# A two-layer decoder trunk on one core: the first stage arranged anew between the two modulation halves, one reading engine for each PSUM bank, and the norm's gain folded into the output weights

## The chip, the core and the metric

The kernel runs on one core of one Trainium2 chip. The metric is the device time of one execution in microseconds (us), as a median over runs; lower is better. The core's engines in the profile are PE (TensorE: matrix products and transposes, with PEld loading its weights), DVE (VectorE), ACT (ScalarE), POOL (GpSimd) and SP (SyncE, which here only issues DMAs). Each engine works through its own row of instructions in order.

## The reference, cut to what matters

```python
for l in range(2):                                   # x: 1024 tokens x 1024
    shift, scale, gate = split(silu(c) @ w_mod[l] + b_mod[l])
    h = rms_norm(x, pre_gain[l]) * (1 + scale) + shift
    proj = h @ w_in[l]                               # 3088 columns
    aq, ak, av, ag, rq, rk, rv, rg, gq, gk, gv, gg, ga = split(proj)
    a_out = sliding_window_attention(rot(aq), rot(ak), av, sinks[l]) * silu(ag)
    r_out = rms_norm(retention(rot(rq), rot(rk), rv)) * silu(rg)
    g     = gated_linear_attention(gq, gk, gv, log_sigmoid(ga @ gw + gb) / 16)
    g_out = rms_norm(g, gla_norm_gain[l]) * silu(gg)  # gain: 64 values, the same for 4 heads
    y = concat(a_out, r_out, g_out) @ w_out[l]        # the last 256 rows of w_out meet g_out
    x = x + gate * rms_norm(y, post_gain[l])
```

`rot` turns pairs by the angle position x frequency; its sine and cosine come from tables that the kernel makes itself.

## The kernel before

**Tiles and products.** Tokens are worked in eight tiles of 128. The columns of W_in are cut into units of 256 (`gg` with the 16 columns of `ga` beside it is 272 wide; then `rg`, `rq`, `rk` and so on; W_out is `o0` to `o3`). Each fp32 operand is held as a high and a low part, and a product of one tile with one unit is three passes (high x high, low x high, high x low) over 8 slices of 128 rows: 24 matmuls at L161 into one PSUM bank. High parts are made by a copy (L473, L475, L577), low parts by subtracting the high part from the original (L478, L561, L581).

**PSUM.** Of the eight banks three are for products (`mm`) and five for transposes and the rest (`aux`); a fourth product has to wait until the readers of the first are done.

**The first stage** (`mod_first`). The modulation of layer 0 needs shift and scale, 1024 values each, from 8 MB of `w_mod`. They come in two halves `hh` of 512 columns. In each half eight row slices `wm` arrive by DMA; PE makes the shift row (`mm<-wm,c_act`), DVE adds up the scale (`acc`; L322 for the first slice, L324 for the others). `finish(hh)` turns both into columns with eight small matmuls against ones, and L304 to L306 on DVE complete them. Only then can the normalised, transposed tiles 0 and 1 be modulated (L571 on ACT, L573 on DVE), split and multiplied. `between(hh, k)` is called after slice k and puts other work there: loading `gg`'s weights ahead of half 1's slices, normalising tiles 0 and 1 (`pre`), loading tiles 2 and 3.

**What follows.** `gg` and `rg` of tiles 0 and 1, then of the pairs 2/3, 4/5, 6/7. `gla_logits` turns a `gg` product into its gate: `silu2` is tanh on ACT (L880) and one DVE operation (L882); a further DVE multiply (L889) puts the norm's gain on it, a DMA stores it, and ACT copies the 16 `ga` columns (L892). The sine and cosine tables are a job (`table_job`, `tables`) of nineteen steps, nearly all on DVE (L411 to L439; two sines on ACT, L435 and L436), that is let in between the gates' steps.

**What sets the order.** PE's order is written by a planner in the code: a clock `clk` adds up matmul costs, jobs are generators that yield a delay from the table `L` or the name of a flag, and `pump()` lets the due ones issue. The other engines take their instructions in the order in which a scheduler puts them, and the two queues that issue DMAs (SP and ACT) are in order too. A DMA also waits for the landing of the one eight before it. `B2` is the number of 2 KB buffers (`t2`), 13; `BST` the number of staging buffers for weights, 5.

## Time and profile before

| | before |
|---|---|
| median of 3 runs | 1011.76 us (1010.34 to 1012.52) |
| the profiled execution | 1013.59 us |
| its span, first to last instruction | 1011.7 us |
| mean granted clock of TensorE | 0.971 |
| busy: PE / DVE / ACT / POOL | 972.2 / 653.4 / 377.4 / 279.7 us |
| matmul and transpose instructions on PE in the profile | 7185 |

The profile shows one execution. Its own time is 1.89 us above its span and 1.83 us above the median of the runs. A row of the timeline gives start, length, engine, source line, operation, output<-inputs and count, and in brackets how long the engine had been idle before and what released it. The granted clock is the share of full speed at which TensorE's array runs.

### The profile page before, as it was taken

What the parts mean: (1) busy time and instruction counts of PE and PEld (TensorE: products, weight loads), DVE (VectorE), ACT (ScalarE), POOL (GpSimd) and SP (SyncE); (2) the same over time, 40 slices, a digit from 0 to 9 for tenths busy, and PEclk for the clock granted to TensorE, in tenths of its full rate; (3) what the DMA queues carried; (4) which work ended last, traced back from release to release, by engine and by line L of the source; (5) the groups of instructions that cost most, each with busy time, mean ns of one, the idle gap of its engine ahead of it and who ended that gap; (6) DMA issues with size and microseconds to landing.
All of it is one profiled execution on the core that took longest, in us unless ns stands there. A gap on an engine that the chain in (4) does not pass through costs nothing.

```text
span 1011.7 us, 19347 instructions
## 1 busy us (share of the span) xinstructions
PE 972.2 (96%) x7185; PEld 845.3 (84%) x7185; DVE 653.4 (65%) x1565; ACT 377.4 (37%) x1050; POOL 279.7 (28%) x310
## 2 busy tenths in 40 slices
PE   5898999999999999999999999999999999999997
PEld 1588999988998877778889999998899887777886
DVE  3789956767757687654478495686575577753322
ACT  2465421232322466632254432132332256662111
POOL 2342201332432154521225120133233124541000
PEclk8899999999899999999999999999988999999999
DMA  9841522443325245678555160153132214455653
GB/s 320 292 123 33 177 69 76 123 130 97 115 86 175 53 138 157 201 246 275 181 166 185 48 183 16 58 168 105 53 95 85 92 46 151 131 164 189 222 189 143
DMA packets 124153, 140.44 MB, mean 139 GB/s; under 512 B 12462, under 2 KB 95384, under 8 KB 124060
## 3 DMA queue, kind: packets, MB, share of 16 engines
q1 hardware_dynamic: 116060, 127.50, 41.0%
q10 hardware_dynamic: 8000, 11.72, 3.3%
q8 instruction: 56, 0.92, 0.4%
q14 instruction: 37, 0.30, 0.1%
HBM read 102.48 MB, written 34.60 MB: 136 GB/s over the span
## 4 chain that ended last, share of the span: by engine, by line
PE 78%; DVE 10%; DMA 5%; ACT 3%; issue 3%; POOL 1%; SPq 0%; ACTq 0%; DVEq 0%; POOLq 0%
PE mm L161 61%; PE aux L161 12%; PE aux L176 4%; DMA st<-in_w_mod_dram 1%; DVE t L573 1%; DVE arena L478 1%; ACT smx L812 1%; POOL sm L514 1%; DMA mixS<-t 1%; DMA xk<-in_x_dram 1%; DMA t<-t 1%; DVE t L544 1%; DVE acc L361 0%; DMA c_freq<-cst_freq_dram 0%; DVE arena L147 0%
## 5 line engine op out<-in xcount | busy, mean ns | idle before, releaser
L161 PE MATMUL mm<-arena,arena 128*128 128x256 f32 (+2 forms) x1824 | 299.9, 320 | 7.1 <-DVE t L882 4.0
L161 PE MATMUL mm<-arena 128*128 128x256 f32 (+2 forms) x1824 | 299.1, 321 | 5.4 <-ACT arena L577 3.0
L161 PEld LDWEIGHTS mm<-arena,arena 128*128 128x128 f32 x1824 | 258.6, 193 | 31.0 <-DVE t L882 4.4
L161 PEld LDWEIGHTS mm<-arena 128*128 128x128 f32 x1824 | 260.7, 195 | 27.9 <-ACT arena L577 3.2
L161 PE MATMUL mm<-arena,mx 128*128 128x512 f32 (+1 forms) x816 | 179.9, 380 | 0.0
L161 PEld LDWEIGHTS mm<-arena,mx 128*128 128x128 f32 x816 | 146.1, 188 | 30.0 <-issue 0.8
L514 POOL TENSOR_TENSOR sm<-sm,mhalf 128x1 f32<-128x1 f32 (+1 forms) x64 | 55.0, 859 | 320.2 <-DVE sm L513 315.8
L478 POOL TENSOR_TENSOR arena<-st,arena 128x512 fp32r<-128x512 f32 x66 | 96.2, 1465 | 102.4 <-ACT arena L145 60.4
L145 ACT ACTIVATE t<-aux 128x512 f32<-128x512 f32 (+1 forms) x96 | 48.4, 519 | 91.2 <-PE aux L161 49.1
L816 POOL TENSOR_TENSOR smx<-smx,sm 128x512 f32<-128x512 f32 x32 | 35.6, 1113 | 112.9 <-DVE sm L815 97.0
L478 DVE TENSOR_TENSOR arena<-st,arena 128x512 fp32r<-128x512 f32 x62 | 61.1, 999 | 4.0 <-PE mm L161 1.7
L145 ACT ACTIVATE arena<-st 128x512 fp32r<-128x512 f32 x90 | 52.5, 624 | 27.3 <-PE mm L161 13.8
L361 DVE SCALAR_TENSOR_TENSOR acc<-st,c_act,acc 128x512 f32<-128x512 f32 x60 | 48.2, 803 | 14.4 <-DMA st<-in_w_mod_dram 13.4
L812 ACT ACTIVATE smx<-smx,sm 128x129 f32<-128x129 f32 x128 | 50.1, 393 | 18.2 <-DVE sm L809 18.0
L176 PE MATMUL aux<-c_ident,t 128*128 128x128 f32 x288 | 47.3, 291 | 7.5 <-DVE t L544 4.4
L1119 ACT ACTIVATE t<-mm 128x512 f32<-128x512 f32 x30 | 18.0, 599 | 93.7 <-PE mm L161 42.6
L1120 DVE TENSOR_TENSOR t<-mm,modg 128x512 f32<-128x512 f32 x30 | 20.7, 688 | 48.8 <-ACT t L1119 48.8
L1155 DVE SCALAR_TENSOR_TENSOR t<-t,sm,t 128x512 f32<-128x512 f32 x32 | 23.8, 777 | 37.1 <-DMA t<-xs 18.8
L176 PEld LDWEIGHTS aux<-c_ident,t 128*128 128x128 f32 x288 | 35.8, 148 | 12.4 <-DVE t L544 5.6
L145 ACT ACTIVATE t<-mm 128x256 f32<-128x256 f32 x40 | 14.9, 379 | 73.6 <-PE mm L161 30.6
L161 PEld LDWEIGHTS aux<-t,mx 32*128 32x128 f32 (+1 forms) x896 | 39.7, 188 | 2.1 <-issue 1.2
L161 PE MATMUL aux<-t,mx 32*128 32x32 f32 (+1 forms) x896 | 40.6, 272 | 0.0
(191 smaller groups left out, 1225.9 us busy)
## 6 DMA issues: line engine op xcount, KB each, us to landing
st<-in_w_in_dram SPq DMA_DIRECT2D x96, 256.0 KB, 3.1
st<-in_w_mod_dram SPq DMA_DIRECT2D x64, 256.0 KB, 3.3
mx<-mixS SPq DMA_DIRECT2D x32, 512.0 KB, 6.5
mixS<-t SPq DMA_DIRECT2D x64, 128.0 KB, 2.7
st<-in_w_out_dram SPq DMA_DIRECT2D x32, 256.0 KB, 2.9
mixS<-t SPq DMA_DIRECT2D x32, 256.0 KB, 2.9
wm<-in_w_mod_dram SPq DMA_DIRECT2D x12, 512.0 KB, 6.1
t<-in_x_dram SPq DMA_DIRECT2D x24, 256.0 KB, 4.6
```

Of the source, the lines that this page charges most:

```text
L145: A.activation(dst, src, AF.Copy)
L161: T.matmul(dst, lhsT, rhs, start=start, stop=stop)
L176: T.transpose(dst, src, idn)
L361: V.scalar_tensor_tensor(acc, wt, c_act[:, k:k + 1], acc, ALU.mult, ALU.add)
L478: (G if first == 0 else eng(f"wlo{kc}")).tensor_tensor(wt[:, 1, 2 * kc:2 * kc + 2, 0:256], st, f(hi), ALU.subtract)
L514: G.tensor_tensor(r, r, mhalf[:, :w], ALU.pow)
L544: V.tensor_scalar(xn[j], xt[j], r, None, ALU.mult)
L812: A.activation(sm[:, h, :], sm[:, h, :], AF.Exp, bias=mx[:, h:h + 1], accum_out=sums[:, h:h + 1])
L816: eng("pn").tensor_tensor(sm[:, :, 0:128], sm[:, :, 0:128], rs.unsqueeze(2).to_broadcast((P, 4, P)), ALU.mult)
L1119: A.activation(yg, pm, AF.Square, accum_out=ss[:, nh:nh + 1])
L1120: V.tensor_tensor(yg, pm, modg[l][:, 512 * nh:512 * nh + 512], ALU.mult)
L1155: V.scalar_tensor_tensor(xt[j], yg[j], r, xt[j], ALU.mult, ALU.add)
```

## The change

1. `load` takes the list of 256-row pieces. `gg`'s first two pieces and its 16 `ga` columns are loaded ahead of half 1's slices, the other two behind them; the low parts of the latter are made on DVE instead of POOL.
2. `between` steps the table generator (`tab`, by the counts in `TAB_N`): eleven steps in half 0, eight in half 1. `table_job` is left with the transposes of the tables.
3. At slice 5 of half 1 `begin` issues eight of the 24 products of `gg` for each of tiles 0 and 1 (high part of `h`, slices 0 to 3); `complete` issues the other sixteen of each after half 1.
4. `pre_early` replaces the early branch of `pre`. Transposes go into four banks: A0, A1 (first halves of tiles 0 and 1) and A2 are read by ACT alone, V2 by DVE alone. ACT modulates slices 4 and 5 and copies their high part, DVE slices 6 and 7 with a copy of its own. The low parts of the first halves (`rest`) are made after half 1's last addition.
5. `rg`'s weights are loaded ahead of x of tiles 2 and 3, and all four of their high parts are made on ACT.
6. In all other `pre`s ACT modulates the first half and DVE the second (`TURN`); before, one slice of the first half and two of the second were ACT's.
7. The multiply by the norm's gain (L889, 16 of them over both layers) goes. The gain is loaded as a column `gncol`, halved, and multiplied into the last two row slices of each unit of W_out while they are split: in the scale of ACT's copy, and in a DVE operation for the low part (eight of them; POOL made them before).
8. `gla_logits` copies `ga` ahead of the tanh. `B2` is 12 instead of 13, and about half of the delays in `L` have other values.

```diff
@@ mod_first
+        rest(0)
         finish(1, row, acc)
@@ load
-    def load(l, name, first=None):
+    def load(l, name, first=None, kcs=range(KT // 2)):
...
+            if name[0] == "o" and kc == 3:
+                gain = gncol[:, l:l + 1]
+                A.activation(hi, st, AF.Copy, scale=gain)
+                V.scalar_tensor_tensor(wt[:, 1, 6:8, 0:256], st, gain, f(hi), ALU.mult, ALU.subtract)
+                continue
             if first == 0:
                 A.activation(hi, st, AF.Copy)
+            elif first == 1 and kc in RG_V:
+                V.tensor_copy(hi, st)
             elif first == 1:
-                V.tensor_copy(hi, st)
+                A.activation(hi, st, AF.Copy)
...
-            (G if first == 0 else eng(f"wlo{kc}")).tensor_tensor(...)
+            (G if first == 0 and kc < 2 else V if first == 0 else eng(f"wlo{kc}")).tensor_tensor(...)
@@
+    def early_products(t, seq, start, stop):
+        w, h = unit(0, "gg"), hT[(0, 0)]
+        c = slice(t * P, t * P + P)
+        for i, (a, b, k) in enumerate(seq):
+            mult(begun[t][:, 0:272], h[:, a, k, c], w[:, b, k, 0:272], start and i == 0, stop and i == len(seq) - 1)
+
+    def begin(t):
+        begun[t] = mm()
+        early_products(t, [(0, b, k) for b in range(2) for k in range(4)], True, False)
+
+    def rest(t):
+        with tc.issue_after(mark[2].ins):
+            V.tensor_tensor(*half.pop(t), ALU.subtract)
+
+    def complete(t):
+        early_products(t, [(1, 0, k) for k in range(4)], False, False)
+        early_products(t, [(a, b, k) for a, b in ((0, 0), (0, 1), (1, 0)) for k in range(4, 8)], False, True)
@@ pre
-                if (j == 0 or k % 2 if early else k in TURN_ACT[j]):
+                if TURN[l][j] == "A":
@@
+    def pre_early(t, xn, h):
+        if t == 0:
+            turns.update({n: aux() for n in ("A0", "A1", "A2", "V2")})
+        for k in range(8):
+            bank = turns[f"A{t}" if k < 4 else "A2" if k % 4 < 2 else "V2"]
...
+        yield (0.0, ("modh", 0, 0))
+        hf = t2()
+        for k in range(4):
+            modulate(A, hf[:, k * P:(k + 1) * P], turns[f"A{t}"][:, k * P:(k + 1) * P], k)
...
+        yield (0.0, ("modh", 0, 1))
+        if t:
+            rest(1)
+        los = []
+        for e, n, k0 in ((A, "A2", 4), (V, "V2", 6)):
...
@@ between
+        for _ in range(TAB_N[8 * hh + k] if k >= 0 else 0):
+            next(tab, None)
+        if hh == 1 and k == BEGIN:
+            begin(0)
+            begin(1)
         if hh == 0 and k == -1:
-            load(0, "gg", 0)
+            load(0, "gg", 0, range(2))
...
         elif hh == 1 and k == -1:
-            for t in (2, 3):
-                load_x(t, xe[t], nc.sync)
+            load(0, "gg", 0, range(2, 4))
@@
+    with tc.issue_after(mark[0].ins), tc.issue_after(mark[1].ins):
+        load(0, "rg", 1)
+    for t in (2, 3):
+        load_x(t, xe[t], nc.sync)
...
-    with tc.issue_after(mark[0].ins), tc.issue_after(mark[1].ins):
-        load(0, "rg", 1)
@@
-    gn5 = cp.tile([P, 2, 64], F32, name="gn5")
...
+    for j in range(2):
+        nc.sync.dma_start(gncol[64 * j:64 * j + 64, :], gn_in.rearrange("a b -> b a"))
+    V.tensor_scalar(gncol, gncol, 0.5, None, ALU.mult)
@@ gla_logits
-        sg = silu2(pg)
-        so = t1()
-        eng("gso").tensor_tensor(h4(so), h4(sg), gn5[:, l].unsqueeze(1).to_broadcast((P, 4, 64)), ALU.mult)
-        dma("ssg", sgS[t], so)
         ga = small(16)
         A.activation(ga, pa, AF.Copy)
+        dma("ssg", sgS[t], silu2(pg))
@@ table_job
-        yield L["tb1"]
-        for _ in tables():
+        for _ in tab:
             yield L["tb2"]
         flag("tables", 2.0)
+        yield L["tb1"]
@@
-B2, B1, BS, BST, MMB, SMB = 13, 8, 11, 5, 3, 6
+B2, B1, BS, BST, MMB, SMB = 12, 8, 11, 5, 3, 6
-TURN_ACT = ((2,), (0, 3))
+TURN = ("AV", "AV")
-L = {"tt1": 6.37, ... "tb1": 24.85, "tb2": 0.52, ... "pf1": 11.01, ... "kv1": 3.07, "kv2": 0.96, ... "fin1": 7.77, ... "pre1@1": 7.74, ...}
+L = {"tt1": 6.51, ... "tb1": 26.69, "tb2": 0.05, ... "pf1": 9.58, ... "kv1": 8.31, "kv2": 2.31, ... "fin1": 11.68, ... "pre1@1": 9.85, ...}
+TAB_N = (0, 1, 1, 2, 1, 1, 1, 1, 2, 2, 1, 3, 0, 0, 0, 0)
+BEGIN = 5
+RG_V = ()
```

Four pieces of the order of instructions. Lines moved with the edits: L544, L571, L573, L577, L473, L478, L880, L882 and L892 of before are, for the early tiles or in general, L573, L613, L614, L621/L635, L479/L483, L486, L944, L946 and L952 of the change, and the table's lines moved by one.

PE around half 1, before (`mm_228` is half 1's shift row, `mm_247` and `mm_285` the columns of halves 0 and 1, `mm_410` and `mm_444` `gg` of tiles 0 and 1, `mm_478` and `mm_508` `rg` of them):

```order
L161 MATMUL mm_228<-wm_224,c_act 1x512 x2
L161 MATMUL mm_247<-c_ones,t_14_122 128x1 x4
L161 MATMUL mm_247<-c_ones,row_123 128x1 x4
L161 MATMUL mm_228<-wm_224,c_act 1x512 x6
L161 MATMUL mm_285<-c_ones,t_42_226 128x1 x4
L161 MATMUL mm_285<-c_ones,row_227 128x1 x4
L161 MATMUL mm_410<-arena_71 128x272 x24
L161 MATMUL mm_444<-arena_71 128x272 x24
L161 MATMUL mm_478<-arena_318,arena_71 128x256 x24
L161 MATMUL mm_508<-arena_318,arena_71 128x256 x7
```

The same stretch now (`mm_232` the shift row, `mm_258` and `mm_323` the columns, `mm_299` and `mm_308` `gg`, `mm_503` and `mm_533` `rg`):

```order
L161 MATMUL mm_232<-wm_228,c_act 1x512 x2
L161 MATMUL mm_258<-c_ones,t_14_123 128x1 x4
L161 MATMUL mm_258<-c_ones,row_124 128x1 x4
L161 MATMUL mm_232<-wm_228,c_act 1x512 x4
L161 MATMUL mm_299<-arena_71 128x272 x8
L161 MATMUL mm_308<-arena_71 128x272 x8
L161 MATMUL mm_232<-wm_228,c_act 1x512 x2
L161 MATMUL mm_323<-c_ones,t_43_230 128x1 x4
L161 MATMUL mm_323<-c_ones,row_231 128x1 x4
L161 MATMUL mm_299<-arena_71 128x272 x16
L161 MATMUL mm_308<-arena_71 128x272 x16
L161 MATMUL mm_503<-arena_361,arena_71 128x256 x24
```

Sixteen of the 48 products of `gg` now stand ahead of half 1's last two slices.

DVE from half 0's columns to half 1's columns, before (`t_42_226` is half 1's `acc`):

```order
L304 TENSOR_TENSOR sm_256<-mm_247,sm_169 128x4
L324 SCALAR_TENSOR_TENSOR t_42_226<-wm_225,c_act,t_42_226 128x512
L305 SCALAR_TENSOR_TENSOR mod_11_119<-sm_256,sm_169 128x4
L306 TENSOR_TENSOR mod_10_118<-mm_247,sm_165 128x4
L324 SCALAR_TENSOR_TENSOR t_42_226<-wm_225,c_act,t_42_226 128x512 x6
L561 TENSOR_TENSOR arena_71<-t_47_260,arena_71 128x4x128
L304 TENSOR_TENSOR sm_294<-mm_285,sm_169 128x4
```

And now, from behind half 0's columns to half 1's (`t_43_230` is half 1's `acc`, `t_48_254` and `sincos` the tables):

```order
L430 SCALAR_TENSOR_TENSOR t_48_254<-t_40_225,t_48_254 128x512 x2
L324 SCALAR_TENSOR_TENSOR t_43_230<-wm_229,c_act,t_43_230 128x512
L430 SCALAR_TENSOR_TENSOR t_48_254<-t_40_225,t_48_254 128x512
L324 SCALAR_TENSOR_TENSOR t_43_230<-wm_229,c_act,t_43_230 128x512
L432 TENSOR_SCALAR t_48_254<-t_48_254 128x512
L324 SCALAR_TENSOR_TENSOR t_43_230<-wm_229,c_act,t_43_230 128x512
L438 SCALAR_TENSOR_TENSOR sincos<-sincos 128x8x64
L324 SCALAR_TENSOR_TENSOR t_43_230<-wm_229,c_act,t_43_230 128x512
L440 TENSOR_SCALAR sincos<-sincos 128x8x64
L324 SCALAR_TENSOR_TENSOR t_43_230<-wm_229,c_act,t_43_230 128x512 x2
L549 TENSOR_TENSOR arena_71<-t_51_271,arena_71 128x4x128
L549 TENSOR_TENSOR arena_71<-t_52_277,arena_71 128x4x128
```

Six steps of the tables stand between the additions to `acc`; behind the last row come two low parts of `gg`'s weights (L486), and then half 1's columns.

DVE at the first gates, now (`sm_401` is the norm of tile 3, `t_87_477` the gate of `mm_299`, whose bank `mm_533` takes):

```order
L573 TENSOR_SCALAR t_70_394<-mx_115,sm_401 128x512
L573 TENSOR_SCALAR t_71_395<-mx_115,sm_401 128x512
L946 SCALAR_TENSOR_TENSOR t_87_477<-t_86_475,mm_299 128x256
L946 SCALAR_TENSOR_TENSOR t_90_500<-t_89_498,mm_308 128x256
L946 SCALAR_TENSOR_TENSOR t_93_530<-t_92_528,mm_503 128x256
```

The three gates stand behind the normalisation of both tiles; before, the first of them (L882) stood ahead of tile 3's.

DVE a little later, where tiles 2 and 3 are modulated, now (`t_98_558` and `t_102_582` are their second halves):

```order
L844 COPY smx_4440<-sink_441 128x4
L591 TENSOR_SCALAR t_98_558<-aux_553,mod_11_120,mod_10_119 128x128 x3
L745 TENSOR_SCALAR gncol<-gncol 128x2
L591 TENSOR_SCALAR t_98_558<-aux_553,mod_11_120,mod_10_119 128x128
L591 TENSOR_SCALAR t_102_582<-aux_577,mod_11_120,mod_10_119 128x128 x3
L596 TENSOR_TENSOR arena_71<-t_98_558,arena_71 128x4x128
L591 TENSOR_SCALAR t_102_582<-aux_577,mod_11_120,mod_10_119 128x128
L946 SCALAR_TENSOR_TENSOR t_104_608<-t_103_606,mm_533 128x256
```

The halving of `gncol`, which waits for the two small DMAs, stands among the modulations; `gn5`'s halving stood there before.

80 lines of the change are left out of this document (49 added, 31 removed).

## The prediction, as it stood before the changed kernel was run

> **What bounds the kernel now.** I read the page's head first, then busy time by stretch, PE's timeline with what released it, and last the other engines' rows at the places where PE waits.
>
> ```profile
> PE 972.2 (96%) x7185; PEld 845.3 (84%) x7185; DVE 653.4 (65%) x1565; ACT 377.4 (37%) x1050; POOL 279.7 (28%) x310
> 75.00:100.00 25.00, 22.14 (x168) 20.24 (x168) 22.76 (x50) 13.47 (x32) 4.79 (x4) 1.00 0.10 33
> 150.00:500.00 350.00, 343.69 (x2620) 295.78 (x2619) 235.98 (x562) 130.78 (x383) 107.92 (x126) 0.98 0.48 146
> 500.00:1012.00 512.00, 501.13 (x3694) 442.16 (x3692) 308.36 (x733) 181.12 (x511) 132.72 (x143) 0.98 0.40 125
> ```
>
> PE is the bound: 972.2 of 1011.7 us. Columns of the other rows: stretch, length, busy time of PE, PEld, DVE, ACT and POOL, PE's granted clock, DMA share, GB/s. The change issues as many products as before, so it can gain only where PE idles or runs at a low clock. From 150 us on PE idles 6.3 and 10.9 us, spread thin. Between 75 and 100 us DVE is fuller than PE (22.76 against 22.14): there DVE is the limit. PE's own rows show the places:
>
> ```profile
> 22.45 5.10 PE L161 MATMUL mm<-wm,c_act 128*1 128x512 f32 x8
> 41.64 7.73 PE L161 MATMUL mm<-arena 128*128 128x272 f32 x44 [2.97 <-ACT arena L577]
> 49.22 3.00 PE L161 MATMUL mm<-arena,arena 128*128 128x256 f32 x25
> 51.83 1.07 PE L161 MATMUL mm<-arena,arena 128*128 128x256 f32 x8
> 59.23 4.80 PE L161 MATMUL mm<-arena 128*128 128x272 f32 x24 [2.46 <-ACT sm L892]
> 63.90 3.27 PE L161 MATMUL mm<-arena 128*128 128x272 f32 x24
> 80.86 2.65 PE L161 MATMUL mm<-arena,arena 128*128 128x272 f32 x16 [0.80 <-POOL arena L581]
> 95.03 3.27 PE L161 MATMUL mm<-arena,arena 128*128 128x272 f32 x24 [1.89 <-DVE t L882]
> 110.80 3.34 PE L161 MATMUL mm<-arena,arena 128*128 128x256 f32 x14 [2.07 <-DVE t L882]
> 39.17:46.00 6.83, 4.36 (x19) 4.36 (x20) 5.26 (x12) 5.10 (x14) 2.33 (x2) 0.50 0.75 233
> 59.65:63.06 3.41, 3.41 (x17) 3.41 (x16) 3.41 (x7) 3.41 (x11) 2.41 (x2) 0.50 0.56 159
> 110.85:114.26 3.41, 3.41 (x16) 3.35 (x17) 3.41 (x11) 0.00 (x0) 0.00 (x0) 0.50 0.77 207
> ```
>
> A product of 272 columns takes 3.27/24 = 0.136 us at full clock and 4.36/19 = 0.23 where the granted clock is 0.50. Half clock lasts whole stretches of 3.41 us and follows a stretch that was mostly idle: 2.46 us of waiting ahead of 59.65, 2.07 ahead of 110.85. The 1.89 us that end at 95.03 lie across two stretches and brought none. So two waits cost more than themselves: 4.80 − 3.27 = 1.5 us at 59.23, and 3.34 − 14 × 0.136 = 1.4 us at 110.80. I use these rows, not a general clock rule, for the sum.
>
> The Trainium skill, "TensorE: Matmul & The Clock Gate", Part 1: The HAM clock gate, has the array fall to half rate after at least one idle window of some 3.4 us and come back after a busy one. The length agrees with 3.41 us. The condition doesn't: the window ahead of 110.85 was busy for a third. By the rule a short wait in front of `gg` of tile 2 costs only itself; by the rows 1.5 us more, which would raise the upper end below by that much, and I go by the rows.
>
> **Half 1's columns come later.** The rows for the first stage:
>
> ```profile
> 31.21 4.68 DVE L324 SCALAR_TENSOR_TENSOR t<-wm,c_act,t 128x512 f32<-128x512 f32 x6
> 38.21 0.16 DVE L305 SCALAR_TENSOR_TENSOR mod<-sm,sm 128x4 f32<-128x4 f32 x1
> 31.33 1.85 ACT L571 ACTIVATE t<-aux,mod,mod 128x128 f32<-128x128 f32 x5 [4.15 <-DVE mod L306]
> 34.78 0.63 ACT L577 ACTIVATE arena<-t 128x512 fp32r<-128x512 f32 x1
> 39.33 1.74 ACT L571 ACTIVATE t<-aux,mod,mod 128x128 f32<-128x128 f32 x4 [3.45 <-DVE t L573]
> 25.52:39.17 13.65, 11.96 (x53) 5.59 (x51) 10.26 (x18) 5.83 (x14) 3.55 (x3) 1.00 1.05 365
> 93.36 0.68 DVE L581 TENSOR_TENSOR arena<-t,arena 128x512 fp32r<-128x512 f32 x1
> 93.96 0.68 DVE L429 SCALAR_TENSOR_TENSOR t<-t,t 128x512 f32<-128x512 f32 x1
> 97.67 0.43 DVE L439 TENSOR_SCALAR sincos<-sincos 128x512 f32<-128x512 f32 x1
> 92.55 1.28 ACT L435 ACT_TABLE_LOAD   x1
> 96.27 0.63 ACT L435 ACTIVATE sincos<-t 128x512 f32<-128x512 f32 x1 [2.44 <-DVE t L431]
> ```
>
> In half 0 the table's steps delay the normalised tiles, but PE is then fed by DMA (the row at 22.45: eight instructions in 5.10 us; the DMA share stands at 1.05 in the stretch from 25.52) and its transposes have slack: I cost those eleven steps at nothing. If that cover were gone, each would cost its 0.4 to 0.7 us.
>
> Two pieces of `gg` no longer stand ahead of half 1's slices: 524,288 bytes, at 365 GB/s 1.4 us. Half 0's columns were ready at 31.3; I take them 1.2 us earlier, at T = 30.1, for DVE's row has table steps in front of them.
>
> From T to the last addition DVE has six L324 (4.68 us), three L430 (0.68 each), L432 (like L439, 0.43), L438 (0.68, by L429's row) and L440 (0.43): 8.3 us. L438 waits for the sines. ACT first does eight modulations and two copies (31.33 to 35.41 in before: 4.1 us), then a table load (1.28) and a sine (0.63), so the sine is there at T + 6.0; DVE comes to it at T + 4.9 and loses 1.1. The last addition ends at T + 9.4 or a little less, since rows overlap by some tenths: 39.3, against 35.9 before. Then four low parts (0.68 each, 2.5 together; two are new on DVE, from POOL) and the column rows stand in DVE's order; PE's sixteen small products (2 us) run beside them. Half 1's columns come at M = 42.05, against 38.37 before: 3.7 us later.
>
> **But less hangs on them.** Before, 44 products stood behind the columns and the first waited till 41.64, 3.3 us, because ACT and DVE read the same banks in turn (3.45 us of idle at 39.33 with DVE named, though its columns were done at 38.37). Now ACT does two modulations of 0.46 and a half-wide copy, and DVE its own bank beside it: the first product at M + 1.4 = 43.45. Of 32 products left four need only old data; 28 wait. At 0.23 us they take 6.4, at 0.136 3.8: end at 47.3 to 49.9. PE idles before them as it did before 41.64, and then half clock held for the 4.4 us to 46.00; with the stretch from 46.0 to 49.4 the first full one, I take 49.7. Before it was 49.22: 0.5 later.
>
> **The next bank is the new wait.** `rg` of tile 0 follows (24 products, some 3 us): 52.7. `rg` of tile 1 needs the bank of `gg` of tile 0, so tanh and L946 behind it. Their queues:
>
> ```profile
> L473 ACT ACTIVATE arena<-st 128x512 fp32r<-128x512 f32 x4 | 2.5, 626 | 3.7 <-DMA st<-in_w_in_dram 3.4
> L529 ACT ACTIVATE t<-mx 128x512 f32<-128x512 f32 x4 | 2.5, 617 | 0.0
> L478 POOL TENSOR_TENSOR arena<-st,arena 128x512 fp32r<-128x512 f32 x6 | 8.0, 1344 | 8.9 <-DMA t<-in_x_dram 5.0 <-DVE sm L513 2.0 <-ACT arena L473 1.9
> L514 POOL TENSOR_TENSOR sm<-sm,mhalf 128x1 f32<-128x1 f32 x4 | 2.9, 724 | 16.6 <-DVE sm L513 16.6
> 52.74 1.91 PE L176 MATMUL aux<-c_ident,t 128*128 128x128 f32 x16
> 54.40 2.25 PE L161 MATMUL mm<-arena,arena 128*128 128x256 f32 x17
> gwt<-in_gla_gate_w_dram SPq DMA_DIRECT2D x2, 8.0 KB, 4.6
> ```
>
> ACT: modulations and copies to M + 2.6, four copies of `rg`'s weights (2.5), four squares (with their reads 2.6): M + 7.7. POOL makes two low parts (1.34 each) and then two roots (0.72). So tile 3 is normalised at M + 10, and L946, behind it in DVE's row, ends at M + 11 = 53.1; with DVE waiting out POOL operations I take 53.6 (bounds 52.7, no wait, and 54.1). From there seven products, sixteen transposes and seventeen products took 51.83 to 56.76 before, 4.9 us: `gg` of tile 2 starts at 58.5. Before it was 59.23 and half clock followed; now the wait is 0.9 us, too short for that: it ends at 58.5 + 3.3 = 61.8 instead of 63.9. **Minus 2.1 us by there.** Loading x of tiles 2 and 3 behind `rg` costs nothing, because ACT comes to the squares only after `rg`'s copies.
>
> L745 waits for the two small `gncol` DMAs. SP issues them behind x of tiles 4 to 7 at 51 to 53; the nearest row, 4.6 us to landing, gives 55.6 to 57.6, and DVE wants it at about 56.5. Queued behind it are the second halves of tiles 2 and 3, for which PE waits. I take 0; bounds 0 and 3 us, with half clock behind it 4.5.
>
> **DVE between 72 and 111 us.** What leaves its row there:
>
> ```profile
> L429 DVE SCALAR_TENSOR_TENSOR t<-t,t 128x512 f32<-128x512 f32 x4 | 3.8, 956 | 0.0
> L420 DVE SCALAR_TENSOR_TENSOR t<-t,t 128x512 f32<-128x512 f32 x4 | 3.8, 950 | 0.0
> L889 DVE TENSOR_TENSOR t<-t,gn 128x256 f32<-128x256 f32 x4 | 1.7, 414 | 0.0
> ```
>
> With the other eleven table steps of 0.4 to 0.7 some 10.6 us of tables, and eight L889 in this layer. So from 75 to 100 DVE would be busy for about 12 of 25 us. The waits at 95.03 and 110.80 name a gate behind table steps (`t L882`); they and the half clock after the second are 1.89 + 2.07 + 1.4 = 5.4 us; with the 0.80 at 80.86, whose low part is POOL's as before, 6.2. What is late next is tanh on ACT, which now has a modulation more in each tile, or POOL's low part. I take **minus 4.0**, bounds 0 and 6.2: the rows at 95.03 and 110.80 in full, the half clock in part gone.
>
> **The rest.** L889 in layer 1, 8 × 0.41 us of DVE; eight low parts of W_out move from POOL to DVE (8 × 0.7); one modulation in each later tile goes from DVE to ACT. None is where PE waits. One `t2` buffer fewer and other delays in `L` move PE's order everywhere. Waits of PE after 125 us look like this, with total, count and longest:
>
> ```profile
> PE aux L176 <- DVE mx L1018: 2.9, 6, 0.6
> PE mm L161 <- DVE t L1132: 2.2, 1, 2.2
> PE aux L161 <- ACT t L145: 2.0, 1, 2.0
> ```
>
> I take **0**, bounds −3 and +5: half of what is there gone, or two more waits of 2.2.
>
> **Sum.** −2.1 − 4.0 + 0 = −6.1 us, on the profiled execution's own 1013.59 (span 1011.7) 1007.5; that execution is 1.8 above the median of the runs shown, so on the median 1011.76 − 6.1 = 1005.7. A measurement of this kernel can tell about 0.2%, 2 us, from no change.
>
> **Rivals.**
> (a) More is won. `gg` ends at 47.3, the bank wait is nothing and all 6.2 come back: start at 57.6, end at 60.9, −3.0 − 6.2, and 1.5 in the later waits: about 1001. For it: DVE's spare time in the table's old place. Against: the idle of PE before half 1's columns.
> (b) No net change. The first stage gives nothing (the end at 63.9 as before, with `gncol` or the bank costing 2 us), and the waits at 95 and 110 return with ACT or POOL named, at half their size, with half clock after them: −2 or so, 1010. For it: the 0.80 on POOL is untouched.
> (c) Slower. The table chain between the halves: L438 holds DVE's row for the sine, behind it stand `acc`, the low parts and half 1's columns. If the sine comes 5 us later than I have it (ACT's modulations late, or its row of `wm` work ahead), M moves to 47 and `gg` ends at 54, so that PE is 4.8 late at 49.22, and the idle before is long enough for half clock to hold through `rg` too (24 × 0.1 more, 2.4). `gg` of tile 2 then starts at 54 + 5.4 + 4.9 = 64.3 and ends, with 24 products at 0.20, at 69.1: +5.2 instead of −2.1. With half of the later 4.0 that is +3.2, 1015. It decides from M = 46. Against: ACT has only 4.1 us ahead of the sine.
> (d) The change doesn't do what it says where DVE's wait for `acc` slices, not its work, fills half 1: then the table would be free there and M earlier; this runs into (a).
>
> **Chances.** The forecast 0.50, (a) with (d) 0.17, (b) 0.23, (c) 0.10. Faster by over 0.2%, below 1009.7: the forecast, (a), and a third of (b): 0.75. Within 0.2%: the rest of (b), 0.15. Slower: 0.10. The likeliest one's own range is 1002 to 1009.5, from the bounds of the two large terms. For 8 in 10 it reaches down to (a)'s 1001 and half of the rest's gain, 1000, and up past (b) to 1012.
>
> **What would show it.** Half 1's columns at about 42, `gg` of tiles 0 and 1 done at about 49.7, a wait for DVE's gate (L946) ahead of `rg` of tile 1 of about 1 us, `gg` of tile 2 starting near 58.5 at clock 1.00; no wait over 1 us for L946 between 75 and 112, and no half clock at 110.85; DVE busy for 11 to 13 us between 75 and 100. A wait named after `gncol`'s halving, or PE idle after 125 us of over 20, would make it wrong.

## The result

| | before | the change |
|---|---|---|
| median of six runs, on one chip | 1011.05 us (1008.06 to 1015.90) | 1005.67 us (1001.48 to 1006.27) |
| ratio, with its 95% interval | 1 | 0.9937 (0.9908 to 0.9966) |
| profiled execution, its span | 1013.59, 1011.7 | 1001.48, 999.8 |

The change is 0.6% faster. The forecast was 1005.7. The profiled execution of the change is the fastest of its six, and that of before is none of its six but slower than five of them, so their spans differ by 11.9 us where the medians differ by 5.4; a second execution of the change (below) has a span of 1004.2.

The head of the page after, then stretches of the span as in the prediction's first fence:

```profile
span 999.8 us, 19316 instructions
PE 965.5 (97%) x7185; PEld 841.0 (84%) x7185; DVE 644.6 (64%) x1545; ACT 385.0 (39%) x1068; POOL 269.2 (27%) x300
75.00:100.00 25.00, 25.00 (x201) 24.05 (x200) 16.70 (x37) 18.47 (x47) 5.91 (x6) 1.00 0.23 74
```

Between 75 and 100 us PE has no gap left (25.00 of 25, before 22.14), and DVE has fallen from 22.76 to 16.70. The timeline of PE, and of DVE where PE's waits come from:

```profile
40.20 1.05 PE L161 MATMUL mm<-c_ones,row 1*128 1x1 f32 x8
43.32 6.15 PE L161 MATMUL mm<-arena 128*128 128x272 f32 x28 [1.31 <-ACT arena L635]
49.31 2.99 PE L161 MATMUL mm<-arena,arena 128*128 128x256 f32 x24
52.87 1.08 PE L161 MATMUL mm<-arena,arena 128*128 128x256 f32 x7 [0.56 <-DVE t L946]
59.22 0.64 PE L161 MATMUL mm<-arena 128*128 128x272 f32 x3 [1.02 <-ACT arena L595]
64.67 1.78 PE L161 MATMUL mm<-arena 128*128 128x272 f32 x12 [0.94 <-DVE arena L596]
101.77 1.06 PE L161 MATMUL mm<-arena,arena 128*128 128x256 f32 x7 [0.38 <-DVE t L946]
35.96 0.69 DVE L438 SCALAR_TENSOR_TENSOR sincos<-sincos 128x512 f32<-128x512 f32 x1 [1.83 <-ACT sincos L436]
41.61 0.16 DVE L305 SCALAR_TENSOR_TENSOR mod<-sm,sm 128x4 f32<-128x4 f32 x1
56.20 0.24 DVE L736 COPY sink<-sm 128x8 f32<-128x8 f32 x2 [2.73 <-DMA sm<-in_attn_sinks_dram]
```

The columns of half 1 are done at 41.77 and `gg` of tiles 0 and 1 at 49.31. The gate waits of 1.89 and 2.07 us are down to one of 0.38. New is the last row: DVE stands still for 2.73 us before L736, and PE's waits of 1.02 and 0.94 us at 59 and 64 come from the modulations behind it (the experiment that loads the sinks earlier shows it).

**A table by stages.** I worked it out from the traces. T is the end of half 0's columns on DVE (L304 to L306). The stages end where PE starts the 145th matmul with split weights (`rg` of tile 2), then the 601st, 901st, 1351st, 2251st, 2401st, 3301st and 3751st matmul into a product bank (`mm`). The gates are the column 145 to 601, and layer 1 begins in the column 2251 to 2401. In two columns the number in brackets is the time in them at a granted clock of 0.50 ("half"). All in us.

| kernel | T | T to 145 | 145 to 601 | 901 to 1351 (half) | 2251 to 2401 | 3301 to 3751 (half) | span |
|---|---|---|---|---|---|---|---|
| before | 31.29 | 36.51 | 60.93 | 104.54 (10.2) | 24.36 | 101.09 (17.1) | 1011.7 |
| change | 29.87 | 36.42 | 55.27 | 107.32 (13.7) | 21.41 | 96.47 (6.8) | 999.8 |
| change, again | 29.89 | 35.90 | 55.75 | 109.24 (17.1) | 21.39 | 97.91 (10.2) | 1004.2 |
| tables back | 29.81 | 34.89 | 58.48 | 108.09 (17.1) | 21.39 | 98.00 (10.2) | 1004.7 |
| gain back | 32.34 | 39.84 | 55.44 | 108.59 (17.1) | 21.37 | 97.71 (10.2) | 1009.2 |
| both back | 30.61 | 35.66 | 59.17 | 107.70 (13.7) | 21.42 | 94.94 (3.4) | 1003.4 |
| no early products | 30.26 | 38.59 | 54.32 | 105.87 (10.2) | 21.38 | 97.13 (10.2) | 1003.5 |
| shared banks | 32.13 | 36.81 | 55.10 | 111.12 (20.5) | 21.38 | 96.48 (6.8) | 1006.5 |
| old delays | 31.78 | 36.86 | 57.37 | 106.35 (13.7) | 26.89 | 99.85 (13.7) | 1011.4 |
| old layer change | 30.22 | 37.36 | 55.09 | 107.00 (13.7) | 24.60 | 96.53 (6.8) | 1002.7 |
| before, new delays | 31.27 | 36.28 | 59.46 | 109.16 (17.1) | 21.89 | 97.98 (10.2) | 1009.4 |
| small loads first | 31.48 | 33.94 | 55.25 | 106.74 (13.7) | 21.40 | 99.19 (13.7) | 1001.3 |
| sine late | 31.36 | 37.04 | 55.09 | 108.07 (17.1) | 21.38 | 98.89 (13.7) | 1004.6 |
| both, and low parts | 30.48 | 32.14 | 55.73 | 105.22 (10.2) | 21.39 | 95.01 (3.4) | 993.1 |

The stage of the gates (145 to 601) repeats within 0.7 us where the code is the same, and the change of layers (2251 to 2401) within 0.1. The first two columns vary by some 2 us, in part with the clock, and the two with half clock go with it at about 0.45 us for each us: that part of a span is chance, and single spans of these kernels differ by more than most edits move. One execution stands apart from all others: one of the twelve of tables back took 1902.72 us, at a granted clock of 1.00; its ratio below leaves it out, and nothing on record explains it.

### The profile page after: what moved, and what is told of

The parts are those of the page before. It is cut to its first block, busy times and chain, and to the rows that moved or that the text cites. A ratio compares the mean times of both kernels' runs of the same rounds, so it can differ in the third digit from the quotient of the medians.

```text
span 999.8 us, 19316 instructions
## 1 busy us (share of the span) xinstructions
PE 965.5 (97%) x7185; PEld 841.0 (84%) x7185; DVE 644.6 (64%) x1545; ACT 385.0 (39%) x1068; POOL 269.2 (27%) x300
## 4 chain that ended last, share of the span: by engine, by line
PE 84%; DMA 6%; DVE 5%; issue 2%; ACT 2%; SPq 1%; POOL 1%; DVEq 0%; POOLq 0%; ACTq 0%
PE mm L161 66%; PE aux L161 13%; PE aux L176 5%; DMA st<-in_w_in_dram 1%; DVE arena L486 1%; DMA st<-in_w_mod_dram 1%; DMA t<-in_x_dram 1%; DMA xk<-in_x_dram 1%; DMA wm<-in_w_mod_dram 1%; DMA sm<-in_attn_sinks_dram 1%; POOL sm L522 1%; DVE t L1216 0%; DMA t<-aoS 0%; DMA t<-srS 0%; SPq L645 0%
## 5 line engine op out<-in xcount | busy, mean ns | idle before, releaser
L161 PEld LDWEIGHTS mm<-arena,mx 128*128 128x128 f32 x816 | 146.2, 188 | 29.8 <-DMA mx<-mixS 0.6
L486 POOL TENSOR_TENSOR arena<-st,arena 128x512 fp32r<-128x512 f32 x56 | 81.9, 1471 | 93.7 <-ACT arena L145 47.1
L880 POOL TENSOR_TENSOR smx<-smx,sm 128x512 f32<-128x512 f32 x32 | 36.1, 1128 | 118.0 <-DVE sm L879 108.8
L486 DVE TENSOR_TENSOR arena<-st,arena 128x512 fp32r<-128x512 f32 x64 | 61.2, 970 | 5.3 <-PE mm L161 3.3
L145 ACT ACTIVATE arena<-st 128x512 fp32r<-128x512 f32 x82 | 48.1, 624 | 29.1 <-PE mm L161 16.9
L1216 DVE SCALAR_TENSOR_TENSOR t<-t,sm,t 128x512 f32<-128x512 f32 x32 | 27.5, 892 | 35.1 <-DMA t<-xs 18.3
```

The costliest lines, as they stand in the source:

```text
L145: A.activation(dst, src, AF.Copy)
L161: T.matmul(dst, lhsT, rhs, start=start, stop=stop)
L486: (G if first == 0 and kc < 2 else V if first == 0 else eng(f"wlo{kc}")).tensor_tensor(wt[:, 1, 2 * kc:2 * kc + 2, 0:256], st, f(hi), ALU. ...
L880: eng("pn").tensor_tensor(sm[:, :, 0:128], sm[:, :, 0:128], rs.unsqueeze(2).to_broadcast((P, 4, P)), ALU.mult)
L1216: V.scalar_tensor_tensor(xt[j], yg[j], r, xt[j], ALU.mult, ALU.add)
```

## The experiments

Medians stand beside the median of before in the same set of runs. The ratios are those on record and not quotients of the two medians (the change again: 0.9922, the quotient would be 0.9938).

| kernel | median, us | before beside it | ratio (95%) |
|---|---|---|---|
| tables back | 1005.99 | 1010.13 | 0.9955 (0.9936 to 0.9974) |
| gain back | 1008.72 | 1010.13 | 0.9989 (0.9975 to 1.0003) |
| no early products | 1007.67 | 1010.13 | 0.9977 (0.9956 to 0.9997) |
| shared banks | 1006.61 | 1010.13 | 0.9956 (0.9932 to 0.9980) |
| change, again | 1006.10 | 1012.38 | 0.9922 (0.9896 to 0.9948) |
| old delays | 1013.00 | 1012.38 | 1.0003 (0.9984 to 1.0023) |
| small loads first | 1002.94 | 1012.38 | 0.9905 (0.9877 to 0.9934) |
| sine late | 1004.99 | 1012.38 | 0.9924 (0.9899 to 0.9948) |
| before, new delays | 1011.11 | 1010.04 | 1.0009 (0.9994 to 1.0023) |
| old layer change | 1007.03 | 1010.04 | 0.9966 (0.9950 to 0.9982) |
| both, and low parts | 1001.56 | 1010.04 | 0.9915 (0.9895 to 0.9934) |
| both back | 1008.37 | 1010.78 | 0.9978 (0.9960 to 0.9997) |

**Tables back.**

```diff
-TAB_N = (0, 1, 1, 2, 1, 1, 1, 1, 2, 2, 1, 3, 0, 0, 0, 0)
+TAB_N = (0,) * 16
@@ table_job
+        yield 24.85
         for _ in tab:
-            yield L["tb2"]
+            yield 0.52
         flag("tables", 2.0)
-        yield L["tb1"]
```

> The change with the nineteen table steps back in the gates' stage (the table job waits 24.85 and steps every 0.52, as before); nothing is stepped between the modulation halves. The front part is read at the start of the 601st matmul into a product bank: 128.73 us before, 121.56 in the change (-7.2). Theory A, room on DVE: of the 7.2 us most came from taking the tables out of DVE's row between 72 and 98 us, so waits for the gate (L946) of 1 us and more return between 80 and 112 and the 601st matmul starts at 125 to 127, although half 1's columns come about 3 us earlier (near 38.5, for no sine is waited for). Theory B, the first stage and the new delays made the gain: the columns come earlier, so the 601st matmul starts at 119 to 121. On the median A gives +3 to +5 against the change, B -1 to -2.

PE's first wait above 1 us in the gates, and the stretch 75 to 100:

```profile
101.85 1.50 PE L161 MATMUL mm<-arena,arena 128*128 128x256 f32 x7 [2.11 <-DVE t L946]
75.00:100.00 25.00, 24.43 (x193) 23.05 (x191) 22.40 (x42) 18.28 (x41) 8.12 (x6) 1.00 0.21 68
```

The 601st matmul starts at 123.18: between the two expectations. Half 1's columns came at 40.16, 1.6 us earlier than in the change and not 3. DVE is full again (22.40), one gate wait of 2.11 us is back with half clock behind it (102.3 to 105.7), and the gates take 58.48 instead of 55.27 to 55.75: 3 us. But the first stage is 1.0 to 1.5 us shorter from T. The move of the tables is worth 3 us where they left and costs about 1.3 where they went. The median is 4.1 below that of before, not clearly apart from the change's.

**Gain back.** The fold in `load` and `gncol` go, `gn5` and the multiply return:

```diff
-            if name[0] == "o" and kc == 3: ...
-        dma("ssg", sgS[t], silu2(pg))
+        sg = silu2(pg)
+        so = t1()
+        eng("gso").tensor_tensor(h4(so), h4(sg), gn5[:, l]..., ALU.mult)
+        dma("ssg", sgS[t], so)
```

> The change with the multiply by the norm's gain back on the gates (16 DVE operations of 0.41 us) and the output weights split as before, without the gain. Theory A, room on DVE: eight of these lie in layer 0's gates and DVE is busy for 16.7 of 25 us from 75 to 100 in the change, so 3.3 us more still fit; the 601st matmul starts at most 1.5 us later than 121.56, and the median moves by 0 to +1.5. Rival: the fold is what took the gate waits away; then waits for a gate of 1 to 2 us return and the start is at 124 or later. The later waits of PE do not change by over 1 us under either.

```profile
63.48 1.53 PE L161 MATMUL mm<-arena 128*128 128x272 f32 x7 [1.82 <-DVE t L941]
70.54 1.67 PE L161 MATMUL mm<-arena 128*128 128x272 f32 x11 [1.65 <-DVE arena L590]
```

Theory A missed. The rival's signs came, a gate wait of 1.82 us and a 601st matmul at 127.62 (2.5 us of that is a later T), but not at the late gates: their stage takes 55.44, as in the change. The loss, 3.4 us, lies ahead of it, at 63 and 70 us, where the first two multiplies (1.49 and 0.41 us) stand in DVE's row among the modulations of tiles 2 and 3 and ahead of the gates that free PE's banks; part of it is half clock during the ones-products in this execution (3.32 us instead of 2.00). The median is 1.4 below before, where the change is 5.4 to 6.3 below.

**Both back.** The two edits together.

> The change with both the table steps and the gain's multiply back in the gates' stage, so that DVE's row there is as full as before, with the first stage, the banks and the delays of the change. Measured from half 0's columns, the 601st product matmul starts 97.4 us later before, 91.7 in the change, 93.4 with the tables back, 95.3 with the gain back. Theory A, DVE's room there is what the front part won: the two add up or more, 97 to 99, with waits for a gate (L941) of 1.5 us and more at two or three places between 80 and 112 as before, and a median 4 to 7 us above the change, which is no faster than before. Theory F, the two undo the same waits: 95 to 96, median 2.5 to 3.5 us above the change.

```profile
92.12 2.41 PE L161 MATMUL mm<-arena,arena 128*128 128x272 f32 x17 [1.05 <-ACT arena L589]
104.20 1.86 PE L161 MATMUL mm<-arena,arena 128*128 128x256 f32 x7 [2.17 <-DVE t L941]
75.00:100.00 25.00, 23.95 (x190) 22.77 (x189) 24.27 (x49) 17.48 (x43) 7.93 (x6) 1.00 0.20 59
```

From T the 601st matmul comes after 94.8 us, just below theory F's 95 to 96 and clearly under A's 97 to 99: the two undo partly the same waits. The gates take 59.17. So room on DVE accounts for 3.7 of the 5.4 us that this stage gained (60.93 to 55.5). The median is 2.4 below before, so some 3 to 4 above the change.

**No early products.** `begin` only takes the bank, `complete` issues all 24.

```diff
-        early_products(t, [(0, b, k) for b in range(2) for k in range(4)], True, False)
...
-        early_products(t, [(1, 0, k) for k in range(4)], False, False)
-        early_products(t, [(a, b, k) for a, b in ((0, 0), (0, 1), (1, 0)) for k in range(4, 8)], False, True)
+        ps_ = ((0, 0), (0, 1), (1, 0))
+        early_products(t, [(a, b, k) for a, b in ps_ for k in range(4)] + [(a, b, k) for a, b in ps_ for k in range(4, 8)], True, True)
```

> The change without the sixteen early products: all 48 products of gg for tiles 0 and 1 stand behind half 1's columns. By A the sixteen (2.4 us between 32.9 and 35.2) run in time in which PE waits for DVE, so without them 16 more products stand behind the columns at half clock: gg of tiles 0 and 1 ends 2 to 3.5 us later than 49.31, at 51.5 to 53, but rg of tile 1 waits for the bank until 52.8 anyway, so of that about 1 to 2.5 us is left at the 601st matmul (122.5 to 124). Rival: DVE's and ACT's queues set the time up to 59 us, the early products only fill waits: 121.5 to 122.

```profile
39.54 1.86 PE L161 MATMUL mm<-c_ones,t 128*128 128x1 f32 x8 [4.44 <-DVE t L324]
59.66 2.59 PE L161 MATMUL mm<-arena,arena 128*128 128x256 f32 x20 [2.39 <-DVE t L945]
```

`gg` ends at 51.90 and the 601st matmul starts at 123.16, 1.6 us later than in the change, as the first theory had it. The first row shows more: without the sixteen products PE idles for 4.4 us, and the ones-products run at half clock, 1.86 + 1.86 us instead of some 1.05 + 1.05. That the missing products brought the half clock is not shown: gain back, shared banks and old delays have them, and their ones-products took 3.3 to 3.6 us too.

**Shared banks.** The second half's modulation as before, each tile's four slices in one bank that ACT and DVE read in turn.

```diff
-        for e, n, k0 in ((A, "A2", 4), (V, "V2", 6)): ...
+        for k in range(4):
+            i = modulate(A if k % 2 else V, hf[...], turns["V2" if t else "A2"][...], 4 + k)
...
+        mark[0] = A.activation(hi, hv, AF.Copy)
+        mark[1] = V.tensor_tensor(h[:, 1, 4:8, tc_], hv, f(hi), ALU.subtract)
```

> The change with half 1's modulation of tiles 0 and 1 as before: each tile's four transposes in one bank that ACT (odd slices) and DVE (even ones) read in turn, one copy of 512 columns on ACT and one low part on DVE for each tile. By my reading of the before's trace (first product 3.3 us behind the columns, against 1.7 in the change) the first product behind the columns starts at 44.8 to 45.2 instead of 43.32, gg ends at 50.5 to 51, and as rg of tile 1 waits until 52.8 for the bank, 0 to 1 us of it is left at the 601st matmul. Rival: the copies and low parts of half width, four instead of two, cost as much on ACT and DVE as the banks save, so nothing moves by over 0.5 us anywhere.

```profile
45.38 0.16 DVE L305 SCALAR_TENSOR_TENSOR mod<-sm,sm 128x4 f32<-128x4 f32 x1
46.02 1.75 ACT L613 ACTIVATE t<-aux,mod,mod 128x128 f32<-128x128 f32 x4 [5.49 <-DVE t L614]
48.34 5.29 PE L161 MATMUL mm<-arena 128*128 128x272 f32 x28 [1.99 <-ACT arena L633]
```

The columns came at 45.54 here, 3.8 later than in the change's first execution (T late, ones-products at half clock). Behind them the first waiting product starts after 2.80 us instead of 1.55: the reading in turn costs 1.25. This is no accident of one execution, for it is 1.55 in all ten executions with the four banks and the early products, and 3.27 in both of the kernels with the old first stage. Hardly any of it goes further: T to 145 is 36.81 against 36.42 and 35.90, because the wait for the bank (0.56 at 57.01) stands behind it. The median does not tell it from the change.

**The change again.** The same kernel in a second execution.

> The change itself, unaltered, timed beside the next three and looked at in a second execution. In the first one the eight ones-products behind half 1's additions ran at full clock (2.0 us) and the half clock began at 41.7; in three of the runs so far they ran at half clock (3.4 to 3.7 us). If the phase of the 3.41 us stretches against the program is chance, this execution may have half 1's columns at 43 to 45.5 and a span of 1002 to 1006 instead of 999.8, with the same order and the same places of waiting; the length of half clock between 200 and 310 and between 690 and 800 us differs by whole stretches, at about 1 to 1.7 us of time each. Rival: the phase belongs to the program; then columns at 41.8 and a span within 1 us of 999.8. Median 1005 to 1006.5 either way.

```profile
39.28 1.02 PE L161 MATMUL mm<-c_ones,t 128*128 128x1 f32 x8 [2.13 <-DVE t L324]
40.23 1.61 PE L161 MATMUL mm<-c_ones,row 1*128 1x1 f32 x8
53.65 1.09 PE L161 MATMUL mm<-arena,arena 128*128 128x256 f32 x7 [1.64 <-DVE t L946]
```

Half clock came within the second group of ones-products (1.61 us instead of 1.05), the columns at 42.24, only half a microsecond later (I had expected 43 to 45.5). The order is the same, the waits are not quite: the wait for the bank is 1.64 instead of 0.56, the one of 1.02 at 59 is missing, and that at 64 is 0.92. Of the 4.4 us between the two spans 3.3 lie in the two marked columns, 1.9 and 1.4, with 3.4 us more of half clock in each. So the phase is chance.

**Old delays.** The table L of before, but for the table job's three numbers.

> The change with all delays of the table L as before, but for the table job's three (tb1, tb2, tt1), and B2 of 12 as in the change. It moves PE's row everywhere; tiles 2 and 3 are transposed behind 21 products of rg of tile 1 instead of 7. Theory A: the delays are the small part; the front part (601st matmul against half 1's columns: 79.8 us in the change, 90.4 before) stays under 82, and the rest (601st to the end: 878.2 in the change, 882.9 before, with 24 and 34 us of half clock in it) is within 2 us of the change's when the half-clock stretches are counted off; median +0 to +2. Rival: the delays made most of the gain; median +3 to +5, with waits that the change does not have.

```profile
106.36 1.09 PE L161 MATMUL mm<-arena,arena 128*128 128x256 f32 x7 [1.60 <-DVE t L946]
540.52 6.27 PE L161 MATMUL mm<-arena,arena 128*128 128x272 f32 x48 [1.30 <-DVE t L1193]
549.90 4.44 PE L161 MATMUL mm<-arena,arena 128*128 128x272 f32 x21 [3.11 <-DVE t L946]
```

My theory fell, and the rival was too small: 1013.0 against 1006.1 for the change beside it, no faster than before. The gates lose 1.9 us, and the change of layers takes 26.89 us instead of 21.4, with waits of 1.30 and 3.11 us.

**Before, with the new delays.** Only L, but for the table job's three numbers, and nothing else of the change.

> The kernel before with the change's table of delays L, but for the three of the table job (tb1, tb2, tt1); nothing else of the change. The change with the old delays came out at 1013.0 (before 1012.4 beside it), so theory D says that the delays, not DVE's room, made the gain: then this is as fast as the change, median -4 to -7 against before, with the wait at the change of layers (2.2 us for the gate t, start 543.4, with half clock behind it) down to about 1.2. Theory E, the delays fit the change's queues and only the two together gain: part of it, -1 to -3, from the change of layers (some 3 us at the 2400th product matmul), while the gate waits at 81, 95 and 110 (4.8 us) stay. A third outcome, slower than before, would say that the new delays alone put products too early.

```profile
59.79 1.95 PE L161 MATMUL mm<-arena 128*128 128x272 f32 x7 [3.15 <-ACT sm L892]
90.23 6.46 PE L161 MATMUL mm<-arena,arena 128*128 128x272 f32 x48 [1.36 <-ACT sm L892]
108.58 1.09 PE L161 MATMUL mm<-arena,arena 128*128 128x256 f32 x7 [1.47 <-DVE t L882]
116.34 3.06 PE L161 MATMUL mm<-arena 128*128 128x256 f32 x24 [1.75 <-DVE t L695]
```

No gain in the median (1.0009), so theory D is out, and E holds for the stages: the change of layers falls to 21.89, while the waits in the gates stay, at other places. What the stages won is not in the median. In this execution the column 901 to 1351 gave back 4.6 us; 6.9 us more of half clock make most of it (at 0.45 each some 3 us), and waits there rose as they did in the change:

```profile
PE aux L176 <- DVE mx L1079: 3.6, 3, 1.9
PE aux L176 <- DVE mx L1018: 1.6, 3, 0.6
PE aux L176 <- DVE mx L1079: 1.7, 3, 0.6
PE aux L176 <- DVE mx L1018: 3.8, 3, 2.0
```

These are PE's waits for `mx` between 180 and 310 us in the change, in before, in old delays and here (total, count, longest). With the new delays PE waits 2 us more there, I think because they put these transposes earlier.

**Old layer change.** Four delays of L as before.

```diff
-"fin1": 11.68, "lay1": 0.07, "pre1@1": 9.85, "lay1@1": 1.23
+"fin1": 7.77, "lay1": 1.23, "pre1@1": 7.74, "lay1@1": 0.9
```

> The change with four delays as before: fin1 7.77 instead of 11.68, pre1@1 7.74 instead of 9.85, lay1 1.23 instead of 0.07, lay1@1 0.9 instead of 1.23; they set when tiles of the next layer are transposed and when the new layer begins. Front part as in the change. In the trace before and with all old delays the stretch between the 2250th and the 2400th product matmul (the change of layers) took 24.4 and 26.9 us, in the change 21.4. If these four made it, it takes 24 to 27 here, a wait of over 2 us for the first gate of layer 1 is back and the median is 2 to 5.5 us above the change. Rival: other delays (gc, kv, mod) shift what stands there; then 21 to 22 us and a median within 1 us.

PE at the first gates of layer 1, in the change, here and in before:

```profile
543.34 3.29 PE L161 MATMUL mm<-arena,arena 128*128 128x272 f32 x24 [1.18 <-DVE t L946]
544.23 4.39 PE L161 MATMUL mm<-arena,arena 128*128 128x272 f32 x21 [2.46 <-DVE t L946]
543.44 8.80 PE L161 MATMUL mm<-arena,arena 128*128 128x272 f32 x56 [2.17 <-DVE t L1132]
```

The stage takes 24.60, the wait is 2.46 with half clock behind it, and the stages around it are as in the change. So these four numbers are worth 3.2 us; the median, 3.0 below before where the change is 5.4 to 6.3 below, agrees.

**Small loads first.** The rows showed a way to go on: L736 waits for a load that stands behind eight others on SP.

```diff
+    sinkn = small(16)
+    nc.sync.dma_start(sinkn, sinks...)
+    for j in range(2):
+        nc.sync.dma_start(gncol[64 * j:64 * j + 64, :], gn_in.rearrange("a b -> b a"))
     for t in range(4, NT):
         job(pre_first(t))
```

> The change with the loads of the sinks and of the norm's gain issued ahead of x of tiles 4 to 7. In the change DVE stands still from 53.5 to 56.2 at L736, which waits for the sinks' landing at 56.15, and the modulations of tiles 2 and 3 behind it make PE wait 1.0 us at 59.2 and 0.9 at 64.7. Theory A: DVE's order made these waits; with the load landed by 53 both go or shrink below 0.3 and the 601st matmul comes 1 to 1.9 us earlier against half 1's columns (78 to 79 us instead of 79.8); median -1 to -2. Rival: ACT's modulations and copies (L589, L595) and POOL's low parts, not L736, set the time, or x of tiles 4 to 7, now issued about 1 us later, is missed: waits of the same length under other names, 79.5 to 80.5, median within 0.5.

```profile
59.16 1.04 PE L161 MATMUL mm<-arena 128*128 128x272 f32 x7
61.94 3.65 PE L161 MATMUL mm<-arena 128*128 128x272 f32 x27
```

Both waits are gone and T to 145 falls by 2.0 to 2.5 us, more than I expected: against half 1's columns the 601st matmul comes after 77.3 us, not 78 to 79. The median is 3.2 lower, but the intervals of the two ratios (0.9905 and 0.9922) overlap, so that it is the stage and not the median that shows the gain.

**Sine late.** L438 and L440 behind the low parts of tiles 0 and 1.

```diff
+    with tc.issue_after(mark[1].ins):
+        for _ in tab:
+            pass
```

> The change with the last two table steps (L438 and L440, which wait for the sines) behind the low parts of tiles 0 and 1 instead of among half 1's additions; the sines themselves stay. In the change L438 idles DVE for 1.83 us and with L440 takes 1.1 more, so the last addition ends at 38.9. Theory A, DVE's row sets half 1's columns: the last addition ends 2.5 to 2.9 us earlier against half 0's columns (T + 6.2 to 6.6 instead of T + 9.0), the columns come 2 to 2.7 earlier, gg of tiles 0 and 1 ends 1.5 to 3 earlier, and 1 to 2.5 of it reaches the 601st matmul; median -1 to -2.5. Rival: PE's shift row and ACT's copy of it (L333, ends at 37.7) take over, so that the columns come less than 1 us earlier, or half clock eats it: median within 0.5.

```profile
39.29 1.05 PE L161 MATMUL mm<-c_ones,t 128*128 128x1 f32 x8 [0.68 <-ACT row L333]
54.28 1.64 PE L161 MATMUL mm<-arena,arena 128*128 128x256 f32 x7 [2.27 <-DVE t L950]
```

The columns come 10.6 us behind T instead of 11.9 and 12.35, less than expected, since PE then waits for ACT's copy of the shift row, as the rival had it. And nothing of it reaches the end: the wait for the bank grows to 2.27, for the two steps now stand in DVE's row ahead of that gate.

**Both, and low parts.** Small loads first, the two steps behind a later gate, and all low parts of `rg`'s weights on DVE, which frees POOL for the roots of tiles 2 and 3.

```diff
-            (G if first == 0 and kc < 2 else V if first == 0 else eng(f"wlo{kc}")).tensor_tensor(...)
+            (G if first == 0 and kc < 2 else V if first is not None else eng(f"wlo{kc}")).tensor_tensor(...)
@@ table_job
+        with tc.issue_after(tgate[0].ins):
+            for _ in tab:
+                pass
```

> The change with the small loads first (as in e7), the two table steps that wait for the sines behind the first gate of rg's second tile, and all four low parts of rg's weights on DVE, so that POOL is free for the roots of tiles 2 and 3. e7 alone gave 1002.9 beside 1006.1. If DVE's row ahead of half 1's columns and POOL's two low parts (4.1 us) hold up the first gate, the columns come 2 to 2.7 us earlier against half 0's, the gate (L946's counterpart) ends 10 to 10.5 us behind them instead of 11.1 to 11.4, and the 601st matmul starts 2 to 3.5 us earlier than with e7 against half 0's columns (e7: 89.2 us): 86 to 87.5; median 1000 to 1001.5. Rival: as with the sine late alone, the earlier columns only lengthen the wait for the bank; then 88.5 to 89.5 and a median of 1002.5 to 1003.5.

```profile
51.68 1.08 PE L161 MATMUL mm<-arena,arena 128*128 128x256 f32 x7 [0.44 <-DVE t L949]
56.35 1.04 PE L161 MATMUL mm<-arena 128*128 128x272 f32 x7
```

The 601st matmul comes 87.87 us behind T (with small loads first alone 89.2, change 91.7), a little short of what I expected. The median of 1001.56 is the lowest of all, 0.85% below before; but the intervals of its ratio, of that of small loads first (0.9905) and of those of the change (0.9922, 0.9937) overlap. The stages up to the 601st matmul are 3.8 us shorter than in the change; that the whole run beats the change is likely and not shown.

## Why the prediction was right, and where it was not

The total was right: 1005.7 forecast, 1005.67 measured, faster at 0.75. Measured against its own before the change won 5.4 us where I had 6.1. Not all of the terms were right, and that the total came so close is in part luck.

- **The first stage to the end of `gg` of tile 2, −2.1.** In the profile `gg` of tile 3 follows at 62.06 (61.8 forecast), before at 63.90: −1.8. The waypoints hold: half 1's columns 41.77 (42.05 forecast), `gg` of tiles 0 and 1 49.31 (49.7), the wait for L946 0.56 (0.9). `gg` of tile 2 began at 57.54, a microsecond ahead of the 58.5, and a wait of 1.02 inside it that I did not have took this back. And 1.4 of the 1.8 is T, which ran from 29.8 to 32.3 in the twelve executions with the new first stage or a variant of it, and from T to the 145th matmul the change wins 0.1 and 0.6. So the first stage as such won next to nothing: the early products (2.2 to 2.7 in this column, a part of it clock) and the banks pay for the tables in it.
- **What stands in DVE's row.** I priced the wait of L745 (`gncol`) at 0. The DMA that DVE waited for was another, the sinks' behind L736, 2.73 us, not in my rows. The chain that I missed starts on SP, which stood for 8.0 us (32.9 to 40.9): the staging buffer for `rg`'s last piece is freed by a low part of `gg` that now stands behind half 1's additions on DVE. The sinks' load, behind that piece and eight loads of x, was issued at 50.87 (before: 43.76):

```profile
SPq L150 <- DVE arena L486: 8.0, 1, 8.0
40.93 0.37 SPq L150 DMA_DIRECT2D st<-in_w_in_dram  x1
47.10 3.73 SPq L645 DMA_DIRECT2D t<-in_x_dram  x8
50.87 0.43 SPq L734 DMA_DIRECT2D sm<-in_attn_sinks_dram  x1
```

- **DVE between 72 and 111 us, −4.0.** The stage of the gates won 5.2 to 5.7 us, near my upper bound of 6.2; nothing took the waits' place. Both back shows 3.7 of it as DVE's room, old delays 1.9 as the planner's. One sign failed: DVE was to be busy for 11 to 13 us between 75 and 100 and was for 16.70. I had only subtracted what leaves; 4.8 us of work that came behind 100 us before (L447, L972 to L1002) moved into the stretch. The 10.6 us of tables were right (10.8 in that stretch), though beside the eight steps shown there are seven others in it and not eleven.
- **The rest, 0.** This is the step that failed, though not its sum. I set the delays in L at nothing "everywhere", within −3 and +5. At the change of layers they are worth −3.0, and two experiments show it from both sides; between 180 and 310 us they cost about 2. And they are not a term that adds: without them the change wins nothing (1.0003), and without the change they win nothing (1.0009). From the 601st matmul to the end before takes 882.9 us with 37.2 of half clock, the change 878.2 with 26.2 and 882.7 with 31.9. With 0.45 us taken off for each us of half clock, 866.2, 866.4 and 868.4 are left: what the change of layers wins beside its half clock is given back elsewhere. So the total came out because larger gains here and in the gates, the smaller one in the first stage and what was given back nearly cancel, and that is luck.
- **Rivals.** (c) did not come: the sine held DVE for 1.83 us (I had 1.1), not 5; it came at T + 6.1, as forecast, and DVE was there 0.6 us earlier. (b)'s POOL wait of 0.80 at 80.86 did not return either.

The spans of the two profiles of the change are 11.9 and 7.5 us below that of before, the medians 5.4 and 6.3. The spans of all executions on record settle this: their mean is 1009.0 over 90 executions of before and 1003.2 over twelve of the change, a difference of 5.8. The profile of before lies 2.7 above its mean, those of the change 3.4 below and 1.0 above theirs. The mean granted clock of these executions is 0.9736 and 0.9765, and among those of before 0.001 of it goes with 0.8 us; by that some 2.3 of the 5.8 us go with less half clock, which is an estimate. How the difference of 5.8 divides over the stages stays open: nothing here averages out the clock stage by stage.

## What to carry to other kernels

Move work off an engine only with its place of arrival priced: here the tables won 3 us in one stage and cost 1.3 in the other. A planner's delays and the queues that they describe are one edit; tried apart, either half can show nothing. When an engine's row is reordered, follow which buffers its late operations free, and what the DMA queue behind them carries.
